# A fused two-layer trunk on one core: mixing loads tied to their pair, first loads in smaller pieces, the residual as a PSUM seed

## The chip, the cores and the metric

The kernel runs on one core of a Trainium2 chip. The metric is the device time of one execution in microseconds (us). The core's engines run each its own list of instructions and wait for each other by semaphores: TensorE (PE in the profile, with PEld for its weight loads), VectorE (DVE), ScalarE (ACT), GpSimd (POOL) and SyncE (SP), which here only issues loads and stores.

## The reference

256 tokens (x is 256 x 2048, fp32) go through one gated MLP layer and one attention layer, each with a norm ahead and a residual addition behind, and a last norm:

```
def gmlp_branch(xn, w_in, v_g, w_s, b_s, w_out):      # layer a
    proj = xn @ w_in                                  # 2048 -> 3 * 4096: u, v, gate
    uv, zg = jax.nn.gelu(proj[..., :8192]), proj[..., 8192:]
    u, v = jnp.split(uv, 2, axis=-1)
    v = rms_norm(v, v_g)
    ws = w_s * causal[None]                           # 16 groups of 128 x 128
    mixed = jnp.einsum('gts,bnsgc->bntgc', ws, vc) + bias
    return (u * mixed * jax.nn.silu(zg)) @ w_out      # 4096 -> 2048

def stick_breaking_branch(xn, w_in, w_out):           # layer b: q, k, v, gate
    q, k, v, zg = jnp.split(xn @ w_in, 4, axis=-1)    # 2048 -> 4 * 2048
    return (stick_breaking_attention(q, k, v) * jax.nn.silu(zg)) @ w_out

h = x
h = h + gmlp_branch(rms_norm(h, norm_g[0]), ...)
h = h + stick_breaking_branch(rms_norm(h, norm_g[1]), ...)
return rms_norm(h, final_g)
```

## The kernel before

The tokens stand as two tiles (NT = 2) of 128 partitions. Every fp32 operand of a large product is split into a high part (hi, fp32r, a cast on ACT) and the rest (lo, a subtraction on DVE); `cut` (L101) does it for weights, two blocks of 128 x 512 at a time, and `terms` (L109) makes three TensorE products of each block: hi by hi, hi by lo and lo by hi. So each 512 KB of weights brings one DMA, one cast of 1.05 us, one subtraction of 1.22 us and twelve products of 512 columns.

The stages follow one another in the program:

- **The start** (L70 to L79): WARM products on a tile of zeros, before any data has come.
- **The first two v columns** (L389 to L411, tiles xr, v_raw, v_hi, v_lo, v_acc): written out by hand for k = 0 to 7, one load of 512 KB for each k (two blocks of columns, index j). For k = 0 the two blocks come in a load each, and x itself (xr) comes in four tiles of four k each; the first quarter of xr is loaded as one piece for k = 0 ahead of the weights, and one piece for k = 1 to 3 behind them. `split_x` (L374) makes x_hi and x_lo of one k.
- **Pairs of columns** (class Pair, L180): two 512-column blocks of the output are computed with seven block products in place of eight, over the first eight k; the products run in the banks a to e of PSUM, and the rest of k follows in `column`. `body` (L235) does the products p6, p2, p7, p3 and p4; between them stand copies from bank to bank on ACT (the last is gu_d<-gu_c, L254) and additions of es on DVE (the last is gu_c<-gu_c, L258). `plus` (L216) adds a second block of weights onto a loaded one by a DMA with an addition, which POOL issues. After `body` the column of j = 0 follows, the column of j = 1 is run in the next pair's `head`.
- **Eight gu pairs** (L516): the gate and u columns of b = 0 to 7. `mixing(b)` (L461) is called at the end of a pair's `body`: it loads the norm gain (vg, spread over all partitions) and two 128 x 128 mixing matrices (ws), both on POOL's queue, cuts the upper half off (affine_select), splits ws into wh and wl and v into vh and vl, and multiplies them into `mix`. Their product with vg, ym, is used when the pair's columns are read out.
- **The product with a_w_out** (o), layer b's qk, bv and bg pairs with the attention's steps in between, and the **final product** with b_w_out (f, L825 to L848): three blocks of 512 columns and two of 256. `finish` adds the residual h, squares it with a sum by row, and multiplies by the final gain gf; `store` makes the norm's factor and scales each 512 columns. h comes back from DRAM (hs) by one DMA of 2 MB (L795).

What sets the order: the program is written with a framework whose scheduler puts each instruction, as early as it thinks it ready, into its engine's list. Where the code wants another order it adds edges that carry no wait: `load` (L172) chains the loads on SP up to the end of the first pair stage, and `issue_after` puts an instruction behind another one. Buffers bound how far loads run ahead: three for weights outside pairs (tag raw), five for hi and lo, five PSUM banks for products.

## Time and profile before

| | |
|---|---|
| three runs | 1169.26, 1171.13, 1172.45 us; median 1171.13 |
| the profiled execution | 1169.53 us, span in the trace 1167.6 us |
| data moved by DMA | 255.8 MB, mean 219 GB/s over the span |
| stages on TensorE | first gu_a product at 167.9 us, first gu_d product at 201.8, first o product at 521.2, first qk product at 703.5 |
| final product on TensorE | first f product at 1070.2 us, last at 1159.3 |

The page divides the span into 40 slices of 29 us; each digit is the busy share of a slice in tenths, PEclk is the clock that TensorE was granted, in tenths of full speed:

```
PE   7999999999999999999999999999999999999997
DVE  5889879999988988966556468988889889796564
ACT  6778677777776867865444446787788787885442
PEclk9999999999999999999999999999999999999999
DMA  8987787787787696466556689776686676727662
```

Two slices of PE are below 9: the first and the last. A timeline row gives start, length, engine, line, operation, output and inputs, and in brackets the idle time before and what ended it.

### The profile page before, as it was taken

What the parts mean: (1) busy time and instruction counts of PE and PEld (TensorE: products, weight loads), DVE (VectorE), ACT (ScalarE), POOL (GpSimd) and SP (SyncE); (2) the same over time, 40 slices, a digit from 0 to 9 for tenths busy, and PEclk for the clock granted to TensorE, in tenths of its full rate; (3) what the DMA queues carried; (4) which work ended last, traced back from release to release, by engine and by line L of the source; (5) the groups of instructions that cost most, each with busy time, mean ns of one, the idle gap of its engine ahead of it and who ended that gap; (6) DMA issues with size and microseconds to landing.
All of it is one profiled execution on the core that took longest, in us unless ns stands there. A gap on an engine that the chain in (4) does not pass through costs nothing.

```text
span 1167.6 us, 14826 instructions
## 1 busy us (share of the span) xinstructions
PE 1150.5 (99%) x5369; PEld 957.8 (82%) x5369; DVE 929.7 (80%) x996; ACT 784.4 (67%) x980; POOL 87.9 (8%) x93
## 2 busy tenths in 40 slices
PE   7999999999999999999999999999999999999997
PEld 5788888888888888888888888888888888888887
DVE  5889879999988988966556468988889889796564
ACT  6778677777776867865444446787788787885442
POOL 2200000121010100000000001001010001100000
PEclk9999999999999999999999999999999999999999
DMA  8987787787787696466556689776686676727662
GB/s 305 334 271 209 225 257 233 194 263 234 194 260 251 173 273 224 119 215 236 195 183 207 211 270 290 196 229 217 184 244 193 176 232 194 203 73 244 234 218 99
DMA packets 129433, 255.80 MB, mean 219 GB/s; under 512 B 8016, under 2 KB 12240, under 8 KB 128848
## 3 DMA queue, kind: packets, MB, share of 16 engines
q1 hardware_dynamic: 117136, 229.67, 58.8%
q0 software_dynamic: 11504, 24.12, 11.7%
...
q8 instruction: 42, 0.69, 0.2%
...
## 4 chain that ended last, share of the span: by engine, by line
PE 91%; DMA 3%; ACT 2%; DVE 2%; issue 2%; SPq 0%; POOLq 0%; POOL 0%; DVEq 0%; ACTq 0%
PE o_acc L110 5%; PE o_acc L112 5%; PE o_acc L111 5%; PE gu_b L111 2%; PE gu_a L111 2%; PE gu_a L112 2%; PE gu_a L110 2%; PE gu_b L110 2%; PE gu_b L112 2%; PE f_acc L112 2%; PE f_acc L111 2%; PE f_acc L110 2%; PE gu_c L111 2%; PE gu_d L112 2%; PE gu_d L111 2%; PE gu_c L110 2%
## 5 line engine op out<-in xcount | busy, mean ns | idle before, releaser
L104 ACT CAST gu_p_hi<-gu_b 128x1024 fp32r<-128x1024 f32 x112 | 115.4, 1051 | 37.4 <-PE gu_c L112 16.8
L315 DVE TENSOR_TENSOR o_lo<-o_raw,o_hi 128x1024 fp32r<-128x1024 f32 x64 | 78.2, 1224 | 75.2 <-ACT o_hi L313 75.1
L106 DVE TENSOR_TENSOR gu_p_lo<-gu_b,gu_p_hi 128x1024 fp32r<-128x1024 f32 x112 | 133.7, 1216 | 3.1 <-ACT gu_p_hi L104 2.7
L313 ACT CAST o_hi<-o_raw 128x1024 fp32r<-128x1024 f32 x64 | 67.2, 1053 | 89.2 <-PE o_acc L112 65.3
L104 ACT CAST gu_hi<-gu_raw 128x1024 fp32r<-128x1024 f32 x64 | 66.5, 1053 | 50.9 <-DMA gu_raw<-in_a_w_in 41.0
L110 PE MATMUL o_acc<-o_hi,yc 128*128 128x512 f32 x256 | 100.4, 392 | 0.0
L111 PE MATMUL o_acc<-o_lo,yc 128*128 128x512 f32 x256 | 99.8, 390 | 0.0
L112 PE MATMUL o_acc<-o_hi,yc 128*128 128x512 f32 x256 | 99.7, 390 | 0.0
L106 DVE TENSOR_TENSOR gu_lo<-gu_raw,gu_hi 128x1024 fp32r<-128x1024 f32 x64 | 77.2, 1220 | 27.2 <-ACT gu_hi L104 27.2
L106 DVE TENSOR_TENSOR qk_p_lo<-qk_b,qk_p_hi 128x1024 fp32r<-128x1024 f32 x56 | 66.7, 1217 | 4.2 <-ACT qk_p_hi L104 4.2
L104 ACT CAST qk_p_hi<-qk_b 128x1024 fp32r<-128x1024 f32 x56 | 57.8, 1050 | 14.9 <-PE o_acc L112 4.2
L106 DVE TENSOR_TENSOR v_lo<-v_raw,v_hi 128x1024 fp32r<-128x1024 f32 x40 | 48.1, 1218 | 24.3 <-ACT v_hi L104 24.2
L104 ACT CAST v_hi<-v_raw 128x1024 fp32r<-128x1024 f32 x40 | 41.6, 1050 | 33.8 <-DMA v_raw<-in_a_w_in 32.1
L315 DVE TENSOR_TENSOR f_lo<-f_raw,f_hi 128x1024 fp32r<-128x1024 f32 x28 | 34.2, 1223 | 30.7 <-ACT f_hi L313 30.6
L112 PEld LDWEIGHTS o_acc<-o_hi,yc 128*128 128x128 f32 x256 | 48.1, 188 | 10.1
L110 PEld LDWEIGHTS o_acc<-o_hi,yc 128*128 128x128 f32 x256 | 48.1, 188 | 9.7
L111 PEld LDWEIGHTS o_acc<-o_lo,yc 128*128 128x128 f32 x256 | 48.1, 188 | 9.7
L110 PE MATMUL f_acc<-f_hi,y_hi 128*128 128x512 f32 (+1 forms) x160 | 55.6, 347 | 0.0
L112 PE MATMUL f_acc<-f_hi,y_lo 128*128 128x512 f32 (+1 forms) x160 | 55.5, 347 | 0.0
L111 PE MATMUL f_acc<-f_lo,y_hi 128*128 128x512 f32 (+1 forms) x160 | 55.5, 347 | 0.0
L106 DVE TENSOR_TENSOR v_p_lo<-v_b,v_p_hi 128x1024 fp32r<-128x1024 f32 x42 | 50.1, 1218 | 4.3 <-ACT v_p_hi L104 4.1
L313 ACT CAST f_hi<-f_raw 128x1024 fp32r<-128x1024 f32 x28 | 29.4, 1051 | 33.0 <-DMA f_raw<-in_b_w_out 24.0
...
## 6 DMA issues: line engine op xcount, KB each, us to landing
...
```

Of the source, the lines that this page charges most:

```text
L104: nc.scalar.copy(hi[:, 0:n], raw[:, 0:n])
L106: nc.vector.tensor_sub(lo[:, 0:n], raw[:, 0:n], f(hi[:, 0:n]))
L110: nc.tensor.matmul(acc, lh, hi, start=first, stop=False, skip_group_check=True)
L111: nc.tensor.matmul(acc, lh, lo, start=False, stop=False, skip_group_check=True)
L112: nc.tensor.matmul(acc, ll, hi, start=False, stop=last, skip_group_check=True)
L313: nc.scalar.copy(hi, raw)
L315: nc.vector.tensor_sub(lo, raw, f(hi))
```

## The change

**Loads and casts of the mixing.** In `mixing` the loads of vg and ws are ordered behind the last of the pair's own accumulating DMAs (`adds[-1]`); the cut of ws and the split into wh and wl are ordered behind the pair's last bank copy on ACT and last addition of es on DVE. Before, the loads were ordered behind the last square of v that had been recorded in `norms` when the function was called, and the casts were free.

**The start.** WARM goes from 13 to 9. For k = 0 `cut` now casts and subtracts each block of 128 x 512 on its own (by=1). x's first quarter comes in four loads of one k each, each ahead of the weights of its k, in place of one load and one of three k.

**The residual.** For the f blocks from the second on, `product` first copies h into the PSUM bank on ACT (seed) and the first product adds to it (start is False); `finish` then reads the sum from PSUM and no longer adds h. h is loaded in four parts. The sum of squares of all blocks but the last is made ahead (`known`), and in `store` the last 256 columns are scaled by the norm's factor and gf in one instruction from PSUM.

The names in the order rows below are the tiles of the code, with numbers that tell buffers apart.

The start, POOL's list from the making of ident to the first norm's factor n_r. Before:

```order
masks.py:197 MEMSET ident 128x128
L467 DMA vg_1701<-in_a_v_norm_g 128x512
L468 DMA ws_1702<-in_wst 128x256
L468 DMA ws_2069<-in_wst 128x256
masks.py:199 ISA
masks.py:199 AFFINE_SELECT ident<-ident 128x128
L469 AFFINE_SELECT ws_1702<-ws_1702 128x256
L468 DMA ws_2436<-in_wst 128x256
L469 AFFINE_SELECT ws_2069<-ws_2069 128x256
L468 DMA ws_2803<-in_wst 128x256
L469 AFFINE_SELECT ws_2436<-ws_2436 128x256
```

After, the same place of POOL's list, up to the first accumulating DMAs of the v pairs:

```order
masks.py:197 MEMSET ident 128x128
masks.py:199 ISA
masks.py:199 AFFINE_SELECT ident<-ident 128x128
L92 TENSOR_TENSOR n_r<-n_ms,half 128x2
L221 DMA v_b_0_439<-in_a_w_in 128x2x512
```

The five loads of the mixing (vg of the first pair and ws of the first four) have left the start. They now stand behind the accumulating DMAs of their own pair; for the first gu pair, POOL after:

```order
L221 DMA gu_b_0_1441<-in_a_w_in 128x2x512
L221 DMA gu_b_1_1443<-in_a_w_in 128x2x512
L471 DMA vg_1697<-in_a_v_norm_g 128x512
L472 DMA ws_1698<-in_wst 128x256
L477 AFFINE_SELECT ws_1698<-ws_1698 128x256
L92 TENSOR_TENSOR nv_r<-nv_ms,half 128x2
```

DVE's list at the start, where x_lo and v_lo are the low parts of x and of the weights. Before:

```order
L378 SCALAR_TENSOR_TENSOR x_lo<-xr_127,cols,x_hi 128x256
L106 TENSOR_TENSOR v_0_lo<-v_0_raw,v_0_hi 128x1024
L474 TENSOR_TENSOR wl_1707<-ws_1702,wh_1706 128x256
L378 SCALAR_TENSOR_TENSOR x_lo<-xr_127,cols,x_hi 128x256 x3
L106 TENSOR_TENSOR v_1_lo<-v_1_raw,v_1_hi 128x1024
L106 TENSOR_TENSOR v_2_lo<-v_2_raw,v_2_hi 128x1024
L474 TENSOR_TENSOR wl_2074<-ws_2069,wh_2073 128x256
```

After:

```order
L383 SCALAR_TENSOR_TENSOR x_lo<-xr_119,cols,x_hi 128x256
L108 TENSOR_TENSOR v_0_lo<-v_0_raw,v_0_hi 128x512 x2
L383 SCALAR_TENSOR_TENSOR x_lo<-xr_119,cols,x_hi 128x256
L108 TENSOR_TENSOR v_1_lo<-v_1_raw,v_1_hi 128x1024
L383 SCALAR_TENSOR_TENSOR x_lo<-xr_119,cols,x_hi 128x256
L108 TENSOR_TENSOR v_2_lo<-v_2_raw,v_2_hi 128x1024
```

Both wl have gone from between the low parts, v_0_lo is made in two halves, and the three x_lo of the first quarter that stood together are spread, one ahead of each v_lo.

The end of the fourth gu pair's `body`. TensorE's list after, from the middle of gu_d's products (L112 to L114 are the three products of `terms`) to the first of column 0:

```order
L112 MATMUL gu_d<-gu_p_hi,x_hi 128x512
L492 MATMUL mix_0_2811<-vh_0_2807,wh_2802 128x256
L493 MATMUL mix_0_2811<-vl_0_2808,wh_2802 128x256
L492 MATMUL mix_1_2824<-vh_1_2820,wh_2802 128x256
L493 MATMUL mix_1_2824<-vl_1_2821,wh_2802 128x256
L113 MATMUL gu_d<-gu_p_lo,x_hi 128x512
L114 MATMUL gu_d<-gu_p_hi,x_lo 128x512
L112 MATMUL gu_d<-gu_p_hi,x_hi 128x512
L113 MATMUL gu_d<-gu_p_lo,x_hi 128x512
L114 MATMUL gu_d<-gu_p_hi,x_lo 128x512
L112 MATMUL gu_a<-gu_08_hi,x_hi 128x512
L112 MATMUL gu_d<-gu_08_hi,x_hi 128x512
```

The next row is the first product with wl. Before, the products in the same pair were those of a later pair's mix and stood in gu_c's block:

```order
L110 MATMUL gu_c<-gu_p_hi,xs_420 128x512
L486 MATMUL mix_0_3916<-vh_0_3912,wh_3908 128x256
L487 MATMUL mix_0_3916<-vl_0_3913,wh_3908 128x256
L488 MATMUL mix_0_3916<-vh_0_3912,wl_3909 128x256
L486 MATMUL mix_0_3916<-vh_0_3912,wh_3908 128x256
L487 MATMUL mix_0_3916<-vl_0_3913,wh_3908 128x256
L488 MATMUL mix_0_3916<-vh_0_3912,wl_3909 128x256
L111 MATMUL gu_c<-gu_p_lo,xs_420 128x512
```

The mix products have moved from an earlier pair into the pair that uses them. DVE's list after, at the same place:

```order
L108 TENSOR_TENSOR gu_p_lo<-gu_b_1_2548,gu_p_hi 128x1024
L260 TENSOR_TENSOR gu_c<-gu_c,gu_es 128x512
L480 TENSOR_TENSOR wl_2803<-ws_2799,wh_2802 128x256
L108 TENSOR_TENSOR gu_08_lo<-gu_08_raw,gu_08_hi 128x1024
L108 TENSOR_TENSOR gu_010_lo<-gu_010_raw,gu_010_hi 128x1024
```

wl stands between the last addition of es and column 0's first low part; on ACT wh stands likewise behind gu_d's copy.

The end of the kernel, DVE's list from the last block's products to the end (nf_r is the norm's factor). Before:

```order
L805 TENSOR_TENSOR h_9111<-f_acc_9805,h_9111 128x256
L808 TENSOR_TENSOR h_9111<-h_9111,gf 128x256
L812 TENSOR_REDUCE nf_tot_9858<-sqf 128x1
L814 TENSOR_SCALAR nf_ms_9860<-nf_tot_9858 128x1
L822 TENSOR_SCALAR h_9111<-h_9111,nf_r_9862 128x512 x3
```

After:

```order
L846 SCALAR_TENSOR_TENSOR h_9107<-f_acc_9745,nf_r_9799,gf 128x256
L835 TENSOR_SCALAR nf_ms_9862<-sqf,nf_pre_9743 128x1
L844 TENSOR_SCALAR h_9107<-h_9107,nf_r_9864 128x512 x2
L844 TENSOR_SCALAR h_9107<-h_9107,nf_r_9864 128x256
L846 SCALAR_TENSOR_TENSOR h_9107<-f_acc_9810,nf_r_9864,gf 128x256
```

Of the second token tile the addition, the product with gf and the reduction have gone, and the third scaling is split in two. (The first row after is the first token tile's last.)

The seeds on ACT, where f_8 to f_14 are the casts of the first f block's weights and y_hi the high parts of the attention's output. After:

```order
L318 CAST f_10_hi<-f_10_raw 128x1024
L310 COPY f_acc_9275<-h_9107 128x512
L310 COPY f_acc_9276<-h_9107 128x512
L782 CAST y_hi<-yf 128x512
L318 CAST f_12_hi<-f_12_raw 128x1024
L782 CAST y_hi<-yf 128x512
L310 COPY f_acc_9429<-h_9107 128x512
L318 CAST f_14_hi<-f_14_raw 128x1024
```

Before, the list at this place had the same casts without the three copies.

The diff, cut to its core (the pair is also handed through `mid` to `mixing`):

```
@@ -15,7 +15,7 @@
 CB = 512
-WARM = 13
+WARM = 9
 KS_A = 4
@@ -98,12 +98,14 @@
-    def cut(raw, n, name):
+    def cut(raw, n, name, by=2):
         hi = wspl.tile([P, 2, CB], F32R, tag="hi", name=f"{name}_hi")
-        nc.scalar.copy(hi[:, 0:n], raw[:, 0:n])
         lo = wspl.tile([P, 2, CB], F32R, tag="lo", name=f"{name}_lo")
-        nc.vector.tensor_sub(lo[:, 0:n], raw[:, 0:n], f(hi[:, 0:n]))
+        for i in range(0, n, by):
+            sl = slice(i, min(i + by, n))
+            nc.scalar.copy(hi[:, sl], raw[:, sl])
+            nc.vector.tensor_sub(lo[:, sl], raw[:, sl], f(hi[:, sl]))
         return hi, lo
@@ -216,7 +218,7 @@
             for g, (k, n) in enumerate(self.groups):
-                nc.gpsimd.dma_start(into[g], self.src(i * self.left.ks + k, n, j), accum_op=ALU.add)
+                adds.append(nc.gpsimd.dma_start(into[g], self.src(i * self.left.ks + k, n, j), accum_op=ALU.add))
@@ -248,17 +250,17 @@
             block(b21, lambda k: left.part(off + k, 0), a, "p2")
-            nc.vector.tensor_add(b, b, es)
+            self.last_dve = nc.vector.tensor_add(b, b, es)
             block(b12, lambda k: left.sum_part(2, k), c, "p7")
             d = self.bank("d")
-            nc.scalar.copy(d, c)
+            self.last_act = nc.scalar.copy(d, c)
             self.minus(b11, b21, b11)
...
             if self.mid is not None:
-                self.mid()
+                self.mid(self)
             for _ in self.column(0):
@@ -299,10 +301,13 @@
-    def product(src, left, ks, name, n=CB, before=None):
+    def product(src, left, ks, name, n=CB, before=None, seed=None):
...
         banks = [ps_acc.tile([P, CB], F32, tag="acc", name=f"{name}_acc{t}") for t in range(NT)]
+        if seed is not None:
+            for t in range(NT):
+                nc.scalar.copy(banks[t][:, 0:n], seed(t))
         m = 2 * CB // n
@@ -317,7 +322,7 @@
                     terms(banks[t][:, 0:n], lh, ll, hi[:, kk, :], lo[:, kk, :],
-                          k0 + kk == ks[0], k0 + kk == ks[-1])
+                          seed is None and k0 + kk == ks[0], k0 + kk == ks[-1])
             tick(2)
@@ -396,13 +399,14 @@
                 load(raw[:, j], w4[:, k, NV + j, :])
-            load(xr[0][:, 1:XC, :], xt[:, 1:XC, :])
         else:
+            if k < XC:
+                load(xr[0][:, k:k + 1, :], xt[:, k:k + 1, :])
             load(raw, w4[:, k, NV:NV + 2, :])
...
         split_x(k)
-        hi, lo = cut(raw, 2, f"v0_{k}")
+        hi, lo = cut(raw, 2, f"v0_{k}", by=1 if k == 0 else 2)
         if k >= 6:
@@ -458,20 +462,22 @@
-        def mixing(b):
+        def mixing(b, pair):
...
-            with tc.issue_after(ins_of(norms[NV - 1])):
+            with tc.issue_after(ins_of(adds[-1])):
                 nc.gpsimd.dma_start(vg, a_v_norm_g[0:1, b * CB:(b + 1) * CB].to_broadcast([P, CB]))
                 nc.gpsimd.dma_start(ws, wst[:, b * GPB:(b + 1) * GPB, :])
-            nc.gpsimd.affine_select(ws, ws, pattern=[[0, GPB], [1, P]], compare_op=ALU.is_ge, fill=0.0,
-                                    base=0, channel_multiplier=-1)
             wh = pb.tile([P, GPB, P], F32R, tag="wh", name=f"wh{b}")
             wl = pb.tile([P, GPB, P], F32R, tag="wl", name=f"wl{b}")
-            nc.scalar.copy(wh, ws)
-            nc.vector.tensor_sub(wl, ws, f(wh))
+            with tc.issue_after(ins_of(pair.last_act)), tc.issue_after(ins_of(pair.last_dve)):
+                nc.gpsimd.affine_select(ws, ws, pattern=[[0, GPB], [1, P]], compare_op=ALU.is_ge, fill=0.0,
+                                        base=0, channel_multiplier=-1)
+                nc.scalar.copy(wh, ws)
+                nc.vector.tensor_sub(wl, ws, f(wh))
             mixed[b] = []
@@ -792,26 +798,41 @@
     h = home("v", [P, NT, D], F32, "h2")
-    nc.sync.dma_start(h, hs)
+    for c in range(NC):
+        nc.sync.dma_start(h[:, :, c * CB:(c + 1) * CB], hs[:, :, c * CB:(c + 1) * CB])
...
     blocks = [(c * CB, CB) for c in range(NC - 1)] + [(D - CB, CH), (D - CH, CH)]
-    sqf = const.tile([P, NT, len(blocks)], F32, name="sqf")
+    NB = len(blocks)
+    sqf = const.tile([P, NT, NB], F32, name="sqf")
+    def residual(i):
+        n0, n = blocks[i]
+        return lambda t: h[:, t, n0:n0 + n]
     def finish(i, t, acc):
+        hb = residual(i)(t)
         n0, n = blocks[i]
-        hs = h[:, t, n0:n0 + n]
-        nc.vector.tensor_add(hs, acc, hs)
+        if i == 0:
+            nc.vector.tensor_add(hb, acc, hb)
+            acc = hb
         junk = pe.tile([P, CB], BF16, tag="junk", bufs=2, name=f"junkf{i}_{t}")
-        nc.scalar.activation(junk[:, 0:n], hs, AF.Square, accum_out=sqf[:, t, i:i + 1])
-        nc.vector.tensor_mul(hs, hs, gf[:, n0:n0 + n])
-
-    def store(t):
+        nc.scalar.activation(junk[:, 0:n], acc, AF.Square, accum_out=sqf[:, t, i:i + 1])
+        if i < NB - 1:
+            nc.vector.tensor_mul(hb, acc, gf[:, n0:n0 + n])
+    def known(t):
         tot = const.tile([P, 1], F32, name=f"nf_tot{t}")
-        nc.vector.tensor_reduce(tot, sqf[:, t, :], axis=mybir.AxisListType.X, op=ALU.add)
+        nc.vector.tensor_reduce(tot, sqf[:, t, 0:NB - 1], axis=mybir.AxisListType.X, op=ALU.add)
+        pre = const.tile([P, 1], F32, name=f"nf_pre{t}")
+        nc.vector.tensor_scalar(pre, tot, 1.0 / D, EPS, op0=ALU.mult, op1=ALU.add)
+        return pre
+    def store(t, pre, acc):
         ms = const.tile([P, 1], F32, name=f"nf_ms{t}")
-        nc.vector.tensor_scalar(ms, tot, 1.0 / D, EPS, op0=ALU.mult, op1=ALU.add)
+        nc.vector.tensor_scalar(ms, sqf[:, t, NB - 1:NB], 1.0 / D, pre, op0=ALU.mult, op1=ALU.add)
         r = const.tile([P, 1], F32, name=f"nf_r{t}")
@@ -819,15 +840,18 @@
             else:
-                nc.vector.tensor_scalar_mul(h[:, t, sl], h[:, t, sl], r)
+                e = min(c * CB + CB, blocks[-1][0])
+                nc.vector.tensor_scalar_mul(h[:, t, c * CB:e], h[:, t, c * CB:e], r)
+                if e < c * CB + CB:
+                    nc.vector.scalar_tensor_tensor(h[:, t, e:], acc, r, gf[:, e:], op0=ALU.mult, op1=ALU.mult)
             (nc.sync if c % 2 == 0 else nc.scalar).dma_start(out[:, t, sl], h[:, t, sl])
...
         acc = product(block_of(b_w_out, n0, n), yl, range(H), f"f{i}", n,
-                      before=lambda k0: drain() if k0 == 8 else None)
+                      before=lambda k0: drain() if k0 == 8 else None, seed=residual(i) if i > 0 else None)
         for t in range(NT):
             finish(i, t, acc[t])
-    i, (n0, n) = len(blocks) - 1, blocks[-1]
+    i, (n0, n) = NB - 1, blocks[-1]
     m = 2 * CB // n
@@ -838,14 +862,16 @@
         last.append((hi, lo))
+    pre = [known(t) for t in range(NT)]
     for t in range(NT):
         acc = ps_acc.tile([P, CB], F32, tag="acc", name=f"f{i}_acc{t}")
+        nc.scalar.copy(acc[:, 0:n], residual(i)(t))
         for k in range(H):
...
             lh, ll = yl.part(k, t)
-            terms(acc[:, 0:n], lh, ll, hi[:, k % m, :], lo[:, k % m, :], k == 0, k == H - 1)
+            terms(acc[:, 0:n], lh, ll, hi[:, k % m, :], lo[:, k % m, :], False, k == H - 1)
         finish(i, t, acc[:, 0:n])
-        store(t)
+        store(t, pre[t], acc[:, 0:n])
```

More of the change, by code (lines that the diff above doesn't have):

```diff
@@ L285, in column @@
                 yield
-    pending = []
+    adds, pending = [], []
     def run(pair):
@@ L385, in evac_v @@
         junk = jk.tile([P, CB], BF16, tag="junk", name=f"junkv{b}_{t}")
-        norms.append(nc.scalar.activation(junk, vs, AF.Square, accum_out=ssq[:, t, 1, b:b + 1]))
+        nc.scalar.activation(junk, vs, AF.Square, accum_out=ssq[:, t, 1, b:b + 1])
     banks = [[ps_acc.tile([P, CB], F32, tag="acc", name=f"v0_acc{t}{j}") for t in range(NT)] for j in range(2)]
@@ L506, in evac_gu, with mid_gu @@
                 nc.vector.tensor_mul(y, y, ym)
-        def mid_gu(b):
+        def mid_gu(b, pair):
             nonlocal rv
@@ L511, in mid_gu @@
                 rv = rstd(1, NV, W, "nv")
-            mixing(b)
+            mixing(b, pair)
             if b == NV - 1:
@@ L517, in trunk_kernel @@
             run(Pair(columns(a_w_in, 2 * W + b * CB, b * CB), left, KD, f"gu{b}", KS_GU,
-                     lambda j, t, bank, b=b: evac_gu(b, j, t, bank), mid=lambda b=b: mid_gu(b)))
+                     lambda j, t, bank, b=b: evac_gu(b, j, t, bank), mid=lambda pair, b=b: mid_gu(b, pair)))
         flush()
```

1 line of the change is left out of this document (removed).

## The prediction

> **What bounds the kernel now.** I read the page's engine table first, then the list of TensorE's waits, then the first 20 us by windows and by timeline, then the last 8 us.
>
> The page's header and engine table (busy us, share of the span, instructions) and the first row of TensorE's list of waits (us in total, times, longest):
>
> ```profile
> span 1167.6 us, 14826 instructions
> PE 1150.5 (99%) x5369; PEld 957.8 (82%) x5369; DVE 929.7 (80%) x996; ACT 784.4 (67%) x980; POOL 87.9 (8%) x93
> PE v_acc L110 <- ACT v_hi L104: 5.4, 2, 4.8
> ```
>
> PE is busy for all but 17 us, and its largest wait stands at the start. The windows of the middle say the same (length, then each engine's busy time and count; granted clock, DMA share and GB/s at the end):
>
> ```profile
> 60.00:100.00 40.00, 40.00 (x178) 33.15 (x177) 35.35 (x33) 29.78 (x39) 2.37 (x2) 1.00 0.85 260
> 200.00:240.00 40.00, 40.00 (x184) 33.27 (x183) 37.66 (x42) 29.11 (x35) 5.79 (x7) 1.00 0.77 222
> ```
>
> 178 products in 40 us are 0.225 us for a 512-column product at the full clock. Between about 50 and 1154 us nothing but fewer products would help, and the change removes none there. So its worth lies in the start and the tail. The start by timeline (start, length, engine, line, operation, count, idle time before and its releaser):
>
> ```profile
> 1.29 4.33 PE L74 MATMUL wps<-warm 128*128 128x512 bf16 x13 [1.29 <-DVE warm L71]
> 1.38 0.72 POOL L467 DMA_DIRECT2D vg<-in_a_v_norm_g  x1 [0.37 <-issue]
> ...
> 3.40 0.15 PEld L74 LDWEIGHTS <-warm 128*128 128x128 bf16 x1 [0.28 <-issue]
> 3.83 0.15 PEld L74 LDWEIGHTS <-warm 128*128 128x128 bf16 x1 [0.28 <-issue]
> ...
> 4.16 0.96 PEld L74 LDWEIGHTS <-warm 128*128 128x128 bf16 x5 [0.18 <-issue]
> ...
> 9.33 1.04 ACT L104 CAST v_hi<-v_raw 128x1024 fp32r<-128x1024 f32 x1 [5.51 <-DMA v_raw<-in_a_w_in]
> ...
> 10.43 1.71 PE L110 MATMUL v_acc<-v_hi,x_hi 128*128 128x512 f32 x4 [4.82 <-ACT v_hi L104]
> ...
> 11.55 0.42 DVE L474 TENSOR_TENSOR wl<-ws,wh 128x256 fp32r<-128x256 f32 x1
> ...
> 14.88 1.09 PE L110 MATMUL v_acc<-v_hi,x_hi 128*128 128x512 f32 x4
> ```
>
> The first real product starts at 10.43 us, since v_hi waits for the weights of k=0. The loads of those two halves, in the view of the tile v_raw (lengths of the issue, first and last start):
>
> ```profile
> L174 SPq DMA_DIRECT2D v_raw<-in_a_w_in x2: 422/422/423, 1.3 to 1.7; - x2
> ...
> DMA to landing us min/median/max: 2.7/5.1/7.5
> ```
>
> The first half landed at 1.25 + 2.7 = 3.95 us, the second, issued 0.47 us later, at 1.73 + 7.5 = 9.26. Windows around them and behind:
>
> ```profile
> 3.00:4.00 1.00, 1.00 (x4) 0.43 (x3) 0.14 (x1) 0.51 (x1) 0.49 (x2) 1.00 0.77 238
> 4.00:5.00 1.00, 1.00 (x6) 0.39 (x4) 0.34 (x1) 0.00 (x0) 0.00 (x0) 1.00 0.44 102
> 10.00:11.00 1.00, 0.57 (x2) 0.52 (x3) 0.59 (x1) 0.92 (x3) 0.41 (x1) 0.94 1.03 414
> 12.00:13.00 1.00, 1.00 (x4) 0.81 (x3) 1.00 (x3) 1.00 (x2) 0.72 (x2) 0.50 0.77 213
> 16.00:20.00 4.00, 4.00 (x19) 3.29 (x18) 4.00 (x9) 2.96 (x7) 1.91 (x2) 1.00 1.02 330
> ```
>
> Between the two landings the rate fell to 102 GB/s with the DMA engines only 44% busy: they were not full, they were held up. What is new in those microseconds is POOL's vg and two ws (issued from 1.38 on), which the program does not need before 190 us. The other loss: the clock column reads 0.50 until about 14.3 us, so products k=0 took 14.88 - 10.43 = 4.45 us where twelve at 0.225 take 2.70.
>
> **The change part by part.**
>
> *Mixing loads away from the start; k=0 cut by halves; x's first quarter in four loads; nine warm-up products.* By POOL's order no DMA of POOL is left before n_r. I take it that the second half then follows the first at the rate of the 10 to 11 us window: 0.262 MB at 414 GB/s is 0.63 us, landing at 4.6. Bounds: 4.6, and 9.26 if POOL's loads were not the cause. A cast of half the width is priced by the 128x512 rows below, 0.62 on ACT, 0.69 on DVE (two halves 0.2 and 0.16 us more than one whole, beside the load of the second). So the first half is cast at 3.95 + 0.65 = 4.6. The warm-up's thirteen products end at 5.62; the last four at the full clock are 4 x 0.22 = 0.88, so nine end at 4.74. The first real product starts there: 10.43 - 4.74 = 5.69 us earlier. The third, on the second half, is asked for at 5.2 and has its cast at 4.6 + 0.65 = 5.3: 0.1 us. With no gap behind the warm-up the clock isn't taken away: 4.45 - 2.70 = 1.75 us. Together 5.69 - 0.1 + 1.75 = **7.3 us**.
>
> The clock may still be low at 4.74: the products were 0.43 us apart (3.40 to 3.83) until about 4.1, and that moment may shift from run to run. Bounds 0 and 1.75 (all that the low clock cost); I take 0.3 off, nearest to this run, where it came before 4.74. The Trainium skill (TensorE: Matmul & The Clock Gate, "Why this matters for your kernels") asks for 4 us or more of busy TensorE; by that the clock would come at 1.29 + 4 = 5.3 and the cost would be (5.3 - 4.74)/2 = 0.3 us, about the sum's. The trace had it in 2.8 us.
>
> The lead must be fed. From k=2 on a step needs two loads of 0.52 MB in 2.70 us, 388 GB/s; 414 suffices, the 330 of 16 to 20 us (with a third ws load in it) doesn't: 3.18 us a step, 0.48 x 6 = 2.9 us lost. SP holds each later load until a buffer of three is free, and that comes with the products, so it moves with them. In before wl (11.55) stood in front of this, and the queue ran dry behind it (213 GB/s at 12 us); both go. I take 414, near the row without POOL's loads, and keep 2.9 as an end. SP issues three more DMAs for x, some 0.43 us each, before loads that wait for buffers anyhow. Later in the v stage two stalls remain:
>
> ```profile
> 38.42 0.50 PE L111 MATMUL v_acc<-v_lo,x_hi 128*128 128x512 f32 x1 [0.67 <-DVE v_lo L106]
> 48.41 0.73 PE L110 MATMUL v_acc<-v_hi,x_hi 128*128 128x512 f32 x2 [0.63 <-ACT v_hi L104]
> ```
>
> I leave them as they are (0); 1.3 us if both go.
>
> *Mixing inside its pair.* Same instructions; wh now stands behind the copy to gu_d on ACT, wl behind gu_c's addition on DVE, the products mix inside gu_d's. In the second pair of before:
>
> ```profile
> 238.40 0.60 POOL L467 DMA_DIRECT2D vg<-in_a_v_norm_g  x1 [21.23 <-DVE ym L490]
> 238.78 0.57 ACT L254 COPY gu_d<-gu_c 128x512 f32<-128x512 f32 x1
> ...
> 240.91 0.40 PE L110 MATMUL gu_d<-gu_p_hi,x_hi 128*128 128x512 f32 x1
> ...
> 242.42 0.69 DVE L258 TENSOR_TENSOR gu_c<-gu_c,gu_es 128x512 f32<-128x512 f32 x1
> ```
>
> wh (0.41, about as wl's 0.42) would be done at 238.78 + 0.57 + 0.41 = 239.8, 1.1 us before gu_d begins. wl would be done at 242.42 + 0.69 + 0.42 = 243.5. By the order the first product with wl comes behind fourteen 512-column and four 256-column products from 240.91 on: 14 x 0.225 + 4 x 0.12 = 3.6, so at 244.5. Slack 1.0 us; behind wl wait gu_08_lo and the casts after it, DVE's whole column, so the cover is thin but there. ws is issued right behind the pair's own additions on POOL, some 15 us ahead. I take 0; bounds -1 (DVE is less jammed) and the rival below.
>
> *The residual in PSUM.* The last half block, its product and what follows it:
>
> ```profile
> 1159.32 0.28 PE L112 MATMUL f_acc<-f_hi,y_lo 128*128 128x256 f32 x1
> 1159.63 0.42 DVE L805 TENSOR_TENSOR h<-f_acc,h 128x256 f32<-128x256 f32 x1 [2.03 <-PE f_acc L112]
> 1160.09 0.42 ACT L807 ACTIVATE junkf<-h 128x256 bf16<-128x256 f32 x1 [3.05 <-DVE h L805]
> 1160.42 0.19 ACT L807 ACTIVATION_READ_ACCUMULATOR junkf<-h 128x1 f32 x1
> 1160.98 0.15 DVE L812 TENSOR_REDUCE nf_tot<-sqf 128x1 f32<-128x5 f32 x1
> 1161.16 0.15 DVE L814 TENSOR_SCALAR nf_ms<-nf_tot 128x1 f32<-128x1 f32 x1
> 1161.40 0.55 POOL L816 TENSOR_TENSOR nf_r<-nf_ms,half 128x1 f32<-128x1 f32 x1 [5.11 <-DVE nf_ms L814]
> 1161.98 1.28 DVE L822 TENSOR_SCALAR h<-h,nf_r 128x512 f32<-128x512 f32 x3 [0.67 <-POOL nf_r L816]
> ```
>
> From the product's end (1159.60) to the scaling 2.38 us. Left of it are the square with its read (0.52), nf_ms (0.15), the power (0.55) and four handovers (0.18): 1.40. The addition, the product with gf and the reduction go: 0.98 us. The last scaling splits in two, some 0.2 for 256 columns and 0.42 as the 256-column addition instead of 0.40: 0.2 more. Net **0.8 us**, bounds 0.5 and 1.0.
>
> The seeds are eight copies on ACT, four of 512 columns (0.57 each like the copy to gu_d) and four of 256, where ACT waits for loads anyhow. Two of them stand before y_hi and f_12_hi and wait for h:
>
> ```profile
> L795 SPq DMA_DIRECT2D h<-hs x1: 460/460/460, 1073.6 to 1073.6; - x1
> DMA to landing us min/median/max: 11.3/11.3/11.3
> 1070.21 0.39 PE L110 MATMUL f_acc<-f_hi,y_hi 128*128 128x512 f32 x1
> 1078.10 0.62 ACT L776 CAST y_hi<-yf 128x512 fp32r<-128x512 f32 x1 [1.89 <-DVE yf L775]
> ...
> 1080.00 1.05 ACT L313 CAST f_hi<-f_raw 128x1024 fp32r<-128x1024 f32 x1 [1.28 <-DMA f_raw<-in_b_w_out]
> ```
>
> TensorE reaches f_12 after six pairs of rows and the transposes between, 1070.2 + 6 x 2.70 + 1 = 1087.4; it is cast at 1080. If the seeds' quarter of h lands halfway (1079) nothing is late. If it lands with the whole (1084.9), f_12 is cast at 1084.9 + 2 x 0.57 + 0.62 + 1.05 = 1087.7 and its low part at 1088.9: up to 1.5 us. I take 0. Three more issues on SP, 1.4 us, delay f_14's load; that one waits behind h's data in any case.
>
> Sum: 7.3 - 0.3 + 0.8 = **7.8 us**. The profiled execution took 1169.53 us (span 1167.6), 1.6 under the median of the runs shown, 1171.13. I forecast halfway between the two: 1169.5 - 7.8 + 0.8 = **1162.5 us**.
>
> **The rivals.**
>
> *Sharing alone* (chance 0.15). The Trainium skill (DMA: Bandwidth & Descriptors, "Queues, rings and completion order") lets each DMA engine take turns between queues packet by packet. As a mechanism of this kernel: POOL's 0.52 MB merely took their share, and the rest of the dip is a slow start of the loads. Then 0.52 / 414 = 1.3 us is saved, the second half lands at 8.0 and is cast at 8.6; TensorE does two products at 4.74 and the other ten from 8.6 to 10.9: 4.0 us gained, 2.3 if the pause of 3.4 us costs the clock. With the tail 3.1 to 4.8: 1165.5 to 1167.2. For it: 5 to 9 us carry both queues' data. Against it: 44% busy engines are not sharing.
>
> *Supply* (0.14): the 330 GB/s case, 7.8 - 2.9 = 4.9: 1165.4.
>
> *Seeds block ACT* (0.04): 1.5 us, 1164.0, inside the range.
>
> *Mixing on TensorE's path* (0.05), the one that ends slower. Place: gu_d in all eight pairs. If DVE reaches wl 2 us later than in the rows, each pair loses 1 us and the gain is gone; from 7.8 / 8 = 0.98 us a pair on it is a loss. At 1.5 us: 12 - 7.8 = 4.2 slower, 1174.5. For it: DVE is 37.66 of 40 us busy there. Against: in before that 94% holds extra mixing work done ahead.
>
> **How the numbers follow.** Forecast 0.62, the rivals as said. Low end: both stalls go and the clock costs nothing, 9.4 us from 1169.3: 1159.8. High end: sharing alone with the clock lost from the median, 1171.1 - 3.1 = 1168.0. Outside lie the slower rival and some of each. A difference of 0.3%, 3.5 us, is about what runs of this kernel can tell from no change (they spread over 3.2): faster is under 1167.6. Forecast, supply, seeds and half of sharing, with a little off: 0.85; within 0.3%: 0.11; slower 0.04.
>
> **What would show it.** Right: the first real product near 4.7 us, two casts of v_hi at 4.0 and 4.7, over 350 GB/s from 4 to 5 us, no clock of 0.50 behind 5 us, k=1 at 7.6; span 1159.8; 7.2 instead of 8.0 us from the last product to the end. Wrong: v_hi's second half after 6 us (sharing); waits on DMA rows between 12 and 30 us (supply); TensorE's waits on wh, wl or gu_08_lo between 190 and 500 us (mixing); a wait near 1087 us (seeds).

## The result and the profile after

| | before | after |
|---|---|---|
| median of the runs | 1172.06 us (6 runs, 1169.26 to 1174.50) | 1162.66 us (6 runs, 1162.23 to 1163.71) |
| the profiled execution | 1169.53 us, span 1167.6 | 1162.46 us, span 1160.6 |

The ratio of the runs is 0.9921, with a 95% interval of 0.9907 to 0.9936: some 9.3 us faster, of which 7.1 us lie between the two profiled executions. The rest is that the profiled execution of before was one of its fast ones (2.5 us under the median), that of after a usual one; part of what before's usual runs lose more is found below, in the step on the mixing.

The page's header and two rows of its engine table, after (busy us, share, instructions):

```profile
span 1160.6 us, 14822 instructions
PE 1148.5 (99%) x5365; PEld 956.2 (82%) x5365; DVE 928.2 (80%) x991; ACT 789.2 (68%) x989; POOL 87.4 (8%) x93
```

TensorE is idle for 12 us in place of 17. The list of TensorE's waits, after (total, times, longest), shows the largest one gone:

```profile
PE wps L74 <- DVE warm L71: 1.3, 1, 1.3
PE v_acc L112 <- ACT v_hi L107: 1.3, 2, 0.9
PE O L727 <- ACT ah L720: 0.8, 1, 0.8
PE v_acc L113 <- DVE v_lo L108: 0.5, 1, 0.5
```

Where before waited 5.4 us for v_hi, after waits 1.3. The start by timeline, after (start, length, engine, line, operation):

```profile
1.29 3.53 PE L74 MATMUL wps<-warm 128*128 128x512 bf16 x9 [1.29 <-DVE warm L71]
...
4.19 0.62 ACT L107 CAST v_hi<-v_raw 128x512 fp32r<-128x512 f32 x1 [0.45 <-DMA v_raw<-in_a_w_in]
...
4.86 0.73 PE L112 MATMUL v_acc<-v_hi,x_hi 128*128 128x512 f32 x2
...
5.83 0.62 ACT L107 CAST v_hi<-v_raw 128x512 fp32r<-128x512 f32 x1 [1.02 <-DMA v_raw<-in_a_w_in]
...
6.50 0.50 PE L112 MATMUL v_acc<-v_hi,x_hi 128*128 128x512 f32 x1 [0.91 <-ACT v_hi L107]
...
8.29 1.05 ACT L107 CAST v_hi<-v_raw 128x1024 fp32r<-128x1024 f32 x1 [0.79 <-DMA v_raw<-in_a_w_in]
...
9.39 1.19 PE L112 MATMUL v_acc<-v_hi,x_hi 128*128 128x512 f32 x4 [0.36 <-ACT v_hi L107]
...
12.61 1.08 PE L112 MATMUL v_acc<-v_hi,x_hi 128*128 128x512 f32 x4
```

The first real product runs at 4.86 instead of 10.43, but the second half of k=0 is cast only at 5.83 and k=1 only at 8.29. Its four hi products start at 9.39 (before 14.88), those of k=2 at 12.61 (before 17.63). From the two traces, the start of the same work:

| | before | after | difference |
|---|---|---|---|
| first product of k=0 | 10.43 | 4.86 | 5.57 |
| first product of k=1 | 14.88 | 9.39 | 5.49 |
| first product of k=2 | 17.63 | 12.61 | 5.02 |
| last product of the first two v columns (v_acc) | 64.08 | 58.00 | 6.08 |
| first product of the first gu pair | 167.89 | 161.81 | 6.08 |
| first product of f | 1070.21 | 1064.03 | 6.18 |
| last product | 1159.32 | 1153.12 | 6.20 |
| end of the span | 1167.62 | 1160.64 | 6.98 |

So 5.0 us come from the start, 1.1 from the rest of the first v columns, 0.1 from the 1000 us between, and 0.8 from the tail. Windows of the start, after (length, busy time and count of each engine; granted clock, DMA share, GB/s):

```profile
3.00:4.00 1.00, 1.00 (x4) 0.42 (x3) 0.22 (x1) 0.51 (x1) 0.00 (x0) 1.00 0.94 300
4.00:5.00 1.00, 0.96 (x5) 0.24 (x3) 0.42 (x2) 0.62 (x1) 0.00 (x0) 1.00 1.10 282
5.00:6.00 1.00, 0.59 (x2) 0.16 (x2) 0.54 (x1) 0.17 (x1) 0.00 (x0) 1.00 0.77 250
6.00:7.00 1.00, 0.50 (x2) 0.46 (x3) 0.52 (x1) 0.46 (x2) 0.00 (x0) 1.00 1.10 355
10.00:12.00 2.00, 1.93 (x9) 1.28 (x8) 1.98 (x3) 1.78 (x3) 0.00 (x0) 1.00 0.98 396
```

The dip of 102 GB/s is gone, and so is the clock of 0.50; but the rate of the first microseconds is 250 to 300 GB/s, not the 414 that the prediction took.

### The profile page after: what moved, and what is told of

Same layout as the page of the kernel before. It is cut to its first block, busy times and chain, and to the rows that moved or that the text cites. A ratio compares the mean times of both kernels' runs of the same rounds, so it can differ in the third digit from the quotient of the medians.

```text
span 1160.6 us, 14822 instructions
## 1 busy us (share of the span) xinstructions
PE 1148.5 (99%) x5365; PEld 956.2 (82%) x5365; DVE 928.2 (80%) x991; ACT 789.2 (68%) x989; POOL 87.4 (8%) x93
## 4 chain that ended last, share of the span: by engine, by line
PE 92%; ACT 2%; DMA 2%; DVE 2%; issue 2%; SPq 0%; POOLq 0%; POOL 0%; DVEq 0%; ACTq 0%
PE o_acc L114 5%; PE o_acc L112 5%; PE o_acc L113 5%; PE gu_a L113 3%; PE gu_a L114 3%; PE gu_b L113 3%; PE gu_a L112 3%; PE gu_b L112 2%; PE gu_b L114 2%; PE f_acc L114 2%; PE f_acc L113 2%; PE f_acc L112 2%; PE gu_d L113 2%; PE gu_d L114 2%; PE gu_c L113 2%; PE gu_d L112 2%
## 5 line engine op out<-in xcount | busy, mean ns | idle before, releaser
L107 ACT CAST gu_p_hi<-gu_b 128x1024 fp32r<-128x1024 f32 x112 | 115.5, 1054 | 35.5 <-PE gu_c L114 15.6
L112 PE MATMUL o_acc<-o_hi,yc 128*128 128x512 f32 x256 | 100.4, 392 | 0.0
L114 PE MATMUL o_acc<-o_hi,yc 128*128 128x512 f32 x256 | 99.7, 390 | 0.0
L108 DVE TENSOR_TENSOR v_lo<-v_raw,v_hi 128x1024 fp32r<-128x1024 f32 (+1 forms) x41 | 48.4, 1196 | 19.7 <-ACT v_hi L107 19.6
L107 ACT CAST v_hi<-v_raw 128x1024 fp32r<-128x1024 f32 (+1 forms) x41 | 41.9, 1030 | 29.2 <-DMA v_raw<-in_a_w_in 27.1
L114 PEld LDWEIGHTS o_acc<-o_hi,yc 128*128 128x128 f32 x256 | 48.1, 188 | 10.0
L112 PEld LDWEIGHTS o_acc<-o_hi,yc 128*128 128x128 f32 x256 | 48.1, 188 | 9.7
L114 PE MATMUL f_acc<-f_hi,y_lo 128*128 128x512 f32 (+1 forms) x160 | 55.5, 347 | 0.0
L112 PE MATMUL f_acc<-f_hi,y_hi 128*128 128x512 f32 (+1 forms) x160 | 55.5, 347 | 0.0
L107 ACT CAST v_p_hi<-v_b 128x1024 fp32r<-128x1024 f32 x42 | 43.1, 1050 | 8.7 <-PE v_c L114 6.1
```

The costliest lines, as they stand in the source:

```text
L107: nc.scalar.copy(hi[:, sl], raw[:, sl])
L108: nc.vector.tensor_sub(lo[:, sl], raw[:, sl], f(hi[:, sl]))
L112: nc.tensor.matmul(acc, lh, hi, start=first, stop=False, skip_group_check=True)
L114: nc.tensor.matmul(acc, ll, hi, start=False, stop=last, skip_group_check=True)
```

## The experiments

Two theories were set against each other: HELD UP (the five mixing loads on POOL's queue held the first weights up, and their leaving is most of the gain) and PIECES (the smaller pieces of the start bring it).

### The three parts alone

Each is the kernel before with one part of the change and nothing of the others. The mixing alone (its loads and casts, `adds`, `last_act`, `last_dve`):

```diff
-            with tc.issue_after(ins_of(norms[NV - 1])):
+            with tc.issue_after(ins_of(adds[-1])):
...
+            with tc.issue_after(ins_of(pair.last_act)), tc.issue_after(ins_of(pair.last_dve)):
```

> The kernel before with the mixing part alone (loads and casts behind the pair's own steps). Theory HELD UP: the five loads on POOL's queue held the second half of the first weights up, and their leaving is most of the gain. Then that half lands near 5.7 us as in the changed kernel, is cast with the first as one 128x1024 piece to 6.8, the first real product starts at 6.9 instead of 10.43, k=1 at 10.0 to 10.3 (behind x's load of three k) instead of 14.88, no clock of 0.50 behind the start; profile 5.0 to 6.2 us shorter than the profiled run of before (1169.53). Rival PIECES: the smaller pieces bring the early start, the five loads only share the rate: second half after 8 us, 0 to 2 us shorter.

The start's pieces alone:

```diff
-WARM = 13
+WARM = 9
...
-        hi, lo = cut(raw, 2, f"v0_{k}")
+        hi, lo = cut(raw, 2, f"v0_{k}", by=1 if k == 0 else 2)
...
-            load(xr[0][:, 1:XC, :], xt[:, 1:XC, :])
+            if k < XC:
+                load(xr[0][:, k:k + 1, :], xt[:, k:k + 1, :])
```

> The kernel before with the start's pieces alone (nine warm-up products, k=0 cut by halves, x's first quarter in four loads); the mixing loads stay at the start. HELD UP: the second half still lands at about 9.3 us; two products at 4.9, the third at 9.9, a pause of over 4 us that costs the clock; k=1 between 13 and 14.5 instead of 14.88: 0.5 to 2 us shorter. PIECES: third product near 6.5 as in the changed kernel, 5 us or more shorter.

The residual's seed alone:

```diff
-                          k0 + kk == ks[0], k0 + kk == ks[-1])
+                          seed is None and k0 + kk == ks[0], k0 + kk == ks[-1])
...
-        store(t)
+        store(t, pre[t], acc[:, 0:n])
```

> The kernel before with the residual's seed alone. From the last product's start to the end of the span 7.5 us instead of 8.3; nothing else moves, so 0.8 us shorter than before on equal starts. Rival: the seeds stand in ACT's way at f_12 near 1087 us and TensorE waits up to 1.5 us there: 0.7 us longer.

| | median us (runs) | to before's 1170.97 (29 runs) | ratio, 95% interval |
|---|---|---|---|
| mixing alone | 1165.96 (5) | -5.0 | 0.9956 (0.9944 to 0.9969) |
| start's pieces alone | 1168.65 (11) | -2.3 | 0.9986 (0.9977 to 0.9995) |
| seed alone | 1170.32 (12) | -0.7 | 0.9997 (0.9987 to 1.0008) |

The three medians add up to 8.0 us, near the whole change's 8.3 against the same median. By the ratios it is 7.1 against 9.3, so the sum is known to some 2 us only. Timeline of the mixing alone, then of the start's pieces alone:

```profile
5.57 1.04 ACT L104 CAST v_hi<-v_raw 128x1024 fp32r<-128x1024 f32 x1 [1.81 <-DMA v_raw<-in_a_w_in]
...
6.66 0.97 PE L110 MATMUL v_acc<-v_hi,x_hi 128*128 128x512 f32 x3 [1.10 <-ACT v_hi L104]
```

```profile
4.96 0.73 PE L112 MATMUL v_acc<-v_hi,x_hi 128*128 128x512 f32 x2
...
8.66 0.62 ACT L107 CAST v_hi<-v_raw 128x512 fp32r<-128x512 f32 x1 [3.76 <-DMA v_raw<-in_a_w_in]
...
9.34 1.22 PE L112 MATMUL v_acc<-v_hi,x_hi 128*128 128x512 f32 x2 [3.64 <-ACT v_hi L107]
```

With the mixing loads away, both halves are there at 5.57, although nothing else of the start is changed, and k=1 starts at 10.11. With all the pieces, but the loads still there, the second half comes at 8.66, TensorE stands still for 3.6 us and k=1 starts at 13.77. PIECES falls as the main cause; the pieces are worth some 2 us of the median.

What the seed alone touches is the tail: 7.64 us from the last product's start (1164.01) to the end of the span (1171.65), 8.30 before. The time cannot resolve 0.7 us; the interval holds no change too. Its profile was taken in its longest run (1173.63), and shows one way in which a run of this kernel gets longer: a load in the o stage came late there.

```profile
539.49 1.04 ACT L316 CAST o_hi<-o_raw 128x1024 fp32r<-128x1024 f32 x1 [8.64 <-DMA o_raw<-in_a_w_out]
...
542.45 1.11 PE L343 MATMUL yT<-ident,v 128*128 128x128 f32 x4 [3.38 <-DVE yc L450]
```

ACT waited 8.64 us for weights, and TensorE 3.38 for what followed; behind that pause the granted clock was 0.50 from 542.0 to 545.4 us. From the first product of o to the first of qk it took 187.3 us here and 182.3 to 182.8 in every other profile. The seed touches nothing in this stage.

### Warm-up in place of the pause

The kernel before with one number changed, WARM = 33.

> The kernel before with 33 warm-up products in place of 13: TensorE has work until about 9.9 us, the first real product stays at 10.43. Theory CLOCK: the pause of 4.8 us takes the clock away for 3.4 us and costs 1.75 us in the best runs, more in others, and so makes the runs of before spread over 5 us. Then no 0.50 stands in the clock record, k=1 starts at 13.1 instead of 14.88, the best run is 1.7 us shorter and the spread is under 2 us as that of the changed kernel (1.5). Rival: the clock is taken away anyhow, or the spread comes from the loads: k=1 at 14.9, spread unchanged.

It did not help: 1172.73 us (12 runs, 1169.81 to 1178.27), ratio 1.0015 (1.0002 to 1.0028). The runs spread over 8.5 us, where under 2 were expected. The clock lasted through the time of before's pause, which the warm-up now fills, and was lost behind the pauses that follow (0.76 and 2.12 us). Windows and timeline of this kernel:

```profile
12.00:16.00 4.00, 1.12 (x3) 0.59 (x3) 3.72 (x6) 4.00 (x9) 1.02 (x2) 0.86 0.89 302
16.00:20.00 4.00, 4.00 (x10) 3.06 (x10) 4.00 (x7) 4.00 (x9) 0.97 (x2) 0.50 0.89 271
```

```profile
10.39 1.31 POOL L469 TENSOR_SCALAR_AFFINE_SELECT ws<-ws 128x256 f32<-128x256 f32 x1 [6.82 <-DMA ws<-in_wst]
...
11.73 0.41 ACT L473 CAST wh<-ws 128x256 fp32r<-128x256 f32 x1 [1.56 <-POOL ws L469]
...
13.25 1.98 ACT L104 CAST v_hi<-v_raw 128x1024 fp32r<-128x1024 f32 x2
...
14.34 0.50 PE L110 MATMUL v_acc<-v_hi,x_hi 128*128 128x512 f32 x1 [2.12 <-ACT v_hi L104]
```

TensorE was busy for 1.12 of the 4 us from 12 to 16, and the clock was 0.50 for the next window. Here a second cost of the mixing at the start is seen: ACT takes its list in order, wh stood in it ahead of x_hi and of k=1's cast, and waited 1.56 us for POOL's cut of ws. So k=1 was cast at 13.25 (before's profile: 11.98). Work for the clock alone is of no use where the next operand is late as well. What the clock by itself cost before is not settled by this run.

### Which load holds the others up

The changed kernel, with loads put back to the start; the casts wh and wl stay in their pair. All of them (vg of the first pair and two ws):

```diff
-            with tc.issue_after(ins_of(adds[-1])):
+            with ExitStack():
                 nc.gpsimd.dma_start(vg, a_v_norm_g[0:1, b * CB:(b + 1) * CB].to_broadcast([P, CB]))
                 nc.gpsimd.dma_start(ws, wst[:, b * GPB:(b + 1) * GPB, :])
```

> The changed kernel with the order of the mixing loads alone undone: vg of the first pair and two ws are issued at the start again (one DMA ahead of its need for the others), the casts wh and wl stay in their pair. Theory LOADS: the transfers themselves hold the second half of the first weights up. Then it is cast near 8.7 us as with the start's pieces alone, over 3 us of TensorE stand still, the clock is taken away behind it, k=1 starts near 13.5 instead of 9.39, and the kernel is 3.5 to 5 us longer than the changed one (1166.2 to 1167.7). Rival CASTS: the loads share and it was wh and wl on ACT and DVE that stood in the way: second half before 7 us, 0 to 1 us longer.

The same with one of the two lines outside the `with`: vg alone, and ws alone.

> The changed kernel with vg's load alone at the start (256 KB, one row of 2 KB read for each of 128 partitions). If the spread load is what holds the others up: nearly all of what the three loads together cost, second half near 8.7 us, 3 to 5 us longer than the changed kernel. If each load costs by its bytes (256 of 512 KB): half of it, second half near 7.2, 1 to 2.5 us longer. If ws is it: under 0.7 us longer.

> The changed kernel with two ws loads at the start (2 x 128 KB, 1 KB a partition) and vg in its pair. The mirror of the run with vg: if vg is what holds up, second half near 6 us and under 0.7 us longer than the changed kernel; if bytes count, half of the three loads' cost; if ws is it, 3 to 5 us longer.

And the first pair's vg by ACT's queue:

```diff
+            if b == 0:
+                nc.scalar.dma_start(vg, a_v_norm_g[0:1, b * CB:(b + 1) * CB].to_broadcast([P, CB]))
             with tc.issue_after(ins_of(adds[-1])):
+                if b > 0:
+                    nc.gpsimd.dma_start(vg, a_v_norm_g[0:1, b * CB:(b + 1) * CB].to_broadcast([P, CB]))
```

> The changed kernel with the first pair's vg load at the start once more, but issued by ACT on its own queue (near 2.8 us) instead of by POOL; the same 256 KB, one row spread over 128 partitions. SPREAD: if it is the spread read that holds the other loads up, the second half of k=0 is again cast near 8 us and the kernel is 2 to 3 us longer than the changed one (1164.7 to 1165.7), as with vg on POOL's queue. POOL'S QUEUE: if it is the way POOL's loads are queued, vg on ACT's queue costs its bytes alone: second half before 6.8 us, under 0.8 us longer (below 1163.5).

| at the start | second half of k=0 cast at | median us | profiled execution |
|---|---|---|---|
| none (the changed kernel) | 5.83 | 1162.66 | 1162.46 |
| vg and two ws, POOL | 8.94 | 1166.26 | 1164.46 |
| vg, POOL | 8.34 | 1165.34 | 1164.77 |
| vg, ACT | 8.38 | 1164.01 | 1164.29 |
| two ws, POOL | 7.26 | 1163.80 | 1163.68 |

LOADS holds and CASTS falls: with the casts in their pair the half still comes at 8.94. By the medians vg on POOL's queue costs 2.7 us and ws 1.1, of the 3.6 that all cost: neither vg alone nor bytes alone. vg delays the half by 2.5 us on either queue, so it isn't POOL's way of queueing (on ACT's queue the first half was late too, cast at 6.74); the time lost by vg on ACT's queue, 1.4 us of the median, is below the 2 to 3 that were expected, though the half is as late. ws, with the same 256 KB, delays by 1.4 us. These delays are of one profile each, and the times mix them with two other things: the clock record turned to full only at 14.16 us with vg on POOL's queue and at 13.07 on ACT's (6.74 with ws), and part of the loss is won back, since the last v_acc product comes at 60.07, 60.06, 59.99 and 59.29 us in the order of the table, against 58.00 in the changed kernel.

The view of the DMA queues from 2 to 9 us (packets, MB, share of 16 engines' time) tells them apart; in turn the changed kernel, vg on POOL's queue, ws, and the kernel before (q1 is SP's queue, q0 POOL's):

```profile
q1 hardware_dynamic: 1053, 2.22, 96.8%
```

```profile
q1 hardware_dynamic: 858, 1.60, 67.8%
q0 software_dynamic: 80, 0.26, 22.8%
```

```profile
q1 hardware_dynamic: 907, 1.69, 76.0%
q0 software_dynamic: 96, 0.26, 13.9%
```

```profile
q1 hardware_dynamic: 627, 1.30, 58.0%
q0 software_dynamic: 153, 0.46, 25.6%
```

A share of 1% of 16 engines over 7 us is 1.12 engine-us, microseconds of one DMA engine. vg took 25.5 engine-us for 0.26 MB, 10 GB/s an engine; ws 15.6, 17 GB/s; SP's loads 2.22 MB in 108, 20 GB/s. On ACT's queue vg took 20.9, 13 GB/s. So the row that is spread over 128 partitions kept the engines busy for 1.6 to 2 times as long as the same bytes of SP's loads; what in that read is slow, no run here shows. The rest of the loss is engines that had nothing: before, the shares add up to 85% (with 1.8% of a third queue), after to 98%. The Trainium skill (DMA: Bandwidth & Descriptors, "Queues, rings and completion order") has each engine take turns between the queues packet by packet; that agrees with both queues slowing each other, and doesn't tell of the idle 15%, which no run here explains.

### The pieces of the start, one by one

The changed kernel with x's first quarter in two loads (the second with three k, ahead of k=1's weights), with 13 warm-up products, with k=0 cast whole (`by=2`), and with k=1 too in two loads and two casts:

> The changed kernel with x's first quarter in two loads again (one k, then three k ahead of the weights of k=1). SUPPLY: from k=1 on the start goes by bytes: 256 KB more stand ahead of v1, 0.7 us at 360 GB/s, so k=1 starts at 10.1 instead of 9.39; two k later all is level but for 0.3 us: 0.2 to 0.7 us longer than the changed kernel. Rival: the three issues saved on SP (0.44 us each) make up for it: the same.

> The changed kernel with 13 warm-up products. FIRST PRODUCT (the prediction's sum, by which the first real product sets the start): 0.9 us longer. SECOND HALF: the warm-up ends at 5.6, but the third product waits for the second half's cast until 6.5 in any case and the two products of 0.45 us fit between, so k=1 starts at 9.4 as before: within 0.2 us of the changed kernel.

> The changed kernel with the weights of k=0 cast in one piece. The cast runs from 5.7 to 6.8, the first product starts there instead of 4.86, with a pause of 2 us behind the warm-up. FIRST PRODUCT: 2 us longer. SUPPLY: twelve products from 6.8 with a short wait for the low part end at 9.8, k=1's cast is done at 9.39 anyhow: 0.3 to 0.6 us longer, half of it caught up by k=2. If the pause costs the clock: 1.7 us more, in some runs.

> The changed kernel with the weights of k=1 too in two loads and two casts, to shorten the wait ahead of k=1 (0.52 us, then 0.23 for the low part). The first half lands some 0.6 us before the whole and its cast takes 0.62 instead of 1.05: k=1 starts at 8.9, right behind k=0. If the products of k=1 stay behind the cast of its second half, or the bytes set k=2 (12.61) anyway, the gain ends there: 0 to 0.7 us shorter than the changed kernel.

| the changed kernel with | first product | k=1 | k=2 | last v_acc product | median us (lowest to highest) |
|---|---|---|---|---|---|
| nothing else | 4.86 | 9.39 | 12.61 | 58.00 | 1162.66 (1162.23 to 1163.71) |
| x in two loads | 4.80 | 10.61 | 13.82 | 58.40 | 1164.93 (1163.13 to 1166.70) |
| 13 warm-up products | 5.38 | 9.25 | 12.45 | 58.03 | 1162.61 (1161.64 to 1164.01) |
| k=0 whole | 6.52 | 11.11 | 13.85 | 58.39 | 1164.43 (1162.81 to 1166.47) |
| k=1 in halves | 4.82 | 8.14 | 10.89 | 57.81 | 1162.49 (1162.17 to 1162.98) |

The changed kernel was not run again beside these. The kernel before was, with medians of 1170.9 and 1171.2 us, against 1172.1 in the runs of the result, so differences of under about 1 us from 1162.66 say little.

- Thirteen warm-up products make the first product 0.5 us later, and nothing else: the wait for the second half takes it up. WARM = 9 is worth nothing here that the runs can tell.
- k=0 cast whole is 1.8 us longer in the median, in its profile (its fastest run) 0.4. Its products of k=0 run at half the clock (below): the pause of 1.2 us behind nine warm-up products came before the clock was granted, at 10.26. Yet this is the fastest run: k=1 is 1.7 us late, and 1.3 of that are won back by the last v_acc product. So the half clock at k=0 is not shown to be the 1.7 us "in some runs" of its expectation; what the longer runs lost was not seen.
- x in two loads cost 2.3 us of the median where 0.2 to 0.7 were expected; in its profile, also its fastest run, 0.7. k=1 was 1.2 us late there. What the longer runs lost was not seen.
- k=1 in halves removes the wait ahead of k=1 (8.14 right behind k=0), is 1.7 us ahead at k=2, and 0.2 at the end of the first v columns: the gain is given back bit by bit (0.7 us are left at 31 us), the last 0.5 at a wait of 0.56 us for a cast at 42.14. No version was found that beats the changed kernel by more than the runs differ.

Timeline of k=0 whole:

```profile
8.39 0.63 PE L113 MATMUL v_acc<-v_lo,x_hi 128*128 128x512 f32 x1
8.82 0.63 PE L114 MATMUL v_acc<-v_hi,x_lo 128*128 128x512 f32 x1
```

## Why the prediction was right, step by step

The forecast was 1162.5 us, the median 1162.66, well inside the range. The mechanism of the start was right, but a nearness of 0.2 us is luck: sizes were off in opposite directions.

- **What bounds the kernel**: as said. Of the 7.0 us of span between these two profiles, 0.1 comes from the 1000 us behind the first v columns.
- **The cause at the start**: shown. The mixing alone brings 5.0 us (part of it later, in the gu pairs, see below), and putting its loads back costs 3.6. "Held up, not sharing" was too sharp: the loads take their share, vg up to twice its bytes' worth, and 15% of the engines' time stands idle besides. The rival of sharing alone, with the second half landing at 8.0, is out: it was cast at 5.83.
- **The size of the start**: 7.0 us were forecast (7.3 less 0.3), 5.0 were there at k=2. The step that failed is the landing of the second half "at the rate of the 10 to 11 us window", 414 GB/s: it was cast at 5.83 in place of 4.6. The lower rate (300, 282 and 250 GB/s from 3 to 6 us) is the smaller part of it: at 280 GB/s its 0.262 MB would have been there 0.94 us behind the first half, which landed at 4.17, so at 5.1. The larger part is that a load does not land at a mean rate. The trace has sixteen completions for it; eight had come by 4.52 us, fourteen by 5.00, and the last came at 5.80. Of k=1's weights eight had come by 6.88, fourteen by 7.44, and the last came at 8.27; so k=1 started at 9.39, not 7.6. That the first product comes at 4.74 was right (4.86), but it sets nothing: with 13 warm-up products it came at 5.38 and the time was the same.
- **The clock**: nothing was lost in this profile, where 0.3 was taken. It can be: with k=0 whole it was granted only at 10.3.
- **Supply later on**: the 2.9 us of the rival did not come. k=2 to k=4 start 2.73 us apart (12.61, 15.34, 18.06), at 347 and 363 GB/s in the windows of 12 to 16 and 16 to 20 us, below the 388 that were asked for. So that demand was too high, and the shortfall was all ahead of k=2.
- **The stalls left at 0 in the first v columns**: 1.1 us were won between k=2 and the last product of these columns, by a term that was put at 0 (a bound of 1.3 was named). That the change brought them is not shown: the seed alone, with the start of before, has none of these waits in its profile, and its last v_acc product comes at 62.66, before's at 64.08, though its k=2 starts 1.1 us later (18.69). In after the timeline has these left, where before had 0.67 and 0.63 besides 0.22:

```profile
32.80 0.50 PE L113 MATMUL v_acc<-v_lo,x_hi 128*128 128x512 f32 x1 [0.53 <-DVE v_lo L108]
...
43.24 0.51 PE L112 MATMUL v_a<-v_p_hi,x_hi 128*128 128x512 f32 x1 [0.21 <-ACT v_p_hi L107]
```

- **Mixing in its pair**: 0 was forecast, and 0.1 gained between these two profiles; no row of TensorE's waits names wh, wl or gu_08_lo. The slower rival did not occur. But before's profile is not a usual one here. From the first gu product to the first of o it took 353.3 us. The three other profiles with the mixing in its old place took 354.9 (start's pieces alone), 354.5 (seed alone) and 354.7 (33 warm-up products), and all ten with the mixing in its pair 353.2. The 1.3 to 1.7 us are lost in the later pairs, mostly where gu_c's products want their low part. On DVE the mixing's ym stands just ahead of it (timeline of the start's pieces alone):

```profile
445.86 1.28 DVE L493 TENSOR_TENSOR ym<-mix,vg 128x512 f32<-128x512 f32 x2
...
447.06 2.35 DVE L108 TENSOR_TENSOR gu_p_lo<-gu_b,gu_p_hi 128x1024 fp32r<-128x1024 f32 x2
...
448.33 0.50 PE L113 MATMUL gu_c<-gu_p_lo,xs 128*128 128x512 f32 x1 [0.16 <-DVE gu_p_lo L108]
```

After, ym stands behind wl and column 0's first low parts, where DVE has idle time. So for a usual run of before the bound of -1 ("DVE is less jammed") was nearer than the 0, and part of the 2.5 us between before's profile and its median is this.
- **The tail**: 0.8 forecast, 0.79 measured (8.30 to 7.51 us behind the last product's start). The rows after:

```profile
1153.12 0.28 PE L114 MATMUL f_acc<-f_hi,y_lo 128*128 128x256 f32 x1
1153.44 0.38 ACT L821 ACTIVATE junkf<-f_acc 128x256 bf16<-128x256 f32 x1 [3.54 <-PE f_acc L114]
1153.72 0.19 ACT L821 ACTIVATION_READ_ACCUMULATOR junkf<-f_acc 128x1 f32 x1
1153.95 0.21 DVE L835 TENSOR_SCALAR nf_ms<-sqf,nf_pre 128x1 f32<-128x1 f32 x1 [3.23 <-ACT junkf L821]
1154.24 0.56 POOL L837 TENSOR_TENSOR nf_r<-nf_ms,half 128x1 f32<-128x1 f32 x1 [5.10 <-DVE nf_ms L835]
...
1154.83 1.14 DVE L844 TENSOR_SCALAR h<-h,nf_r 128x512 f32<-128x512 f32 x3 [0.67 <-POOL nf_r L837]
```

The scaling starts 1.71 us behind the last product's start; before it was 2.66.

- **The seeds**: ACT did stand in front of h for 5.26 us, and had slack for it.

```profile
1073.81 1.11 ACT L310 COPY f_acc<-h 128x512 f32<-128x512 f32 x2 [5.26 <-DMA h<-hs]
...
1075.38 1.05 ACT L318 CAST f_hi<-f_raw 128x1024 fp32r<-128x1024 f32 x1
```

f_12 is cast at 1076.4; by the prediction's count TensorE asks for it at 1064.0 + 17.2 = 1081.2, and nothing waited there.

- **Sum and median**: 7.0 us of span against 7.8; the profiled execution of before lay 2.5 us under the median of six runs, and the forecast had added 0.8 for that, where the changed kernel's profile needed 0.2. So 0.7 too much gain and 0.6 too much added time meet, by luck; and in the 7.0 the start's shortfall of 2.0 is already halved by the 1.1 that was put at 0.
